# Low parts of split weights: a negated high part and an adding transfer in place of a subtraction

## The chip, the cores and the metric

The kernel runs on one core of a Trainium2 chip. The metric is device time in microseconds (us), the median of three runs. The core has five engines that work side by side, each through its own instructions in order: PE (TensorE, matmuls; PEld is its weight load), DVE (VectorE), ACT (ScalarE), POOL (GpSimd) and SP (SyncE, which here only issues transfers). Sixteen DMA engines move data between memory and the core's on-chip memory (SBUF); SP, ACT and POOL each have a queue that issues to them.

## The reference

One inference step of a hybrid diffusion backbone, two layers over 640 tokens (512 latent, 128 context) of 1024 features:

```
h  = RMSNorm(x) * (1 + scale1) + shift1
z  = h @ w_in                                # 6688 columns for all branches
x += gate1 * (sum_b sigmoid(G_b) * (branch_b @ w_b)) @ w_o   # linear attention, short convolution, Fourier mixing
h  = RMSNorm(x) * (1 + scale2) + shift2
gate, up = split(h @ w_up)
x += gate2 * (silu(gate) * up) @ w_down      # D_FF = 2816
```

The modulation vectors (shift, scale, gate) are `SiLU(cond) @ w_ada + b_ada`. All arrays are float32. The outputs are the normed tokens and the final attention states.

## The kernel before

**Products in three parts.** PE multiplies in a reduced format (fp32r). To keep float32 precision, each operand is split into a high part, the value cast to that format, and a low part, the value minus the high part. A product is then three matmuls of 128 x 128 weights by 320 tokens: high by high, high weight by low token, low weight by high token (`mm3`, lines 224 to 226, and `dense`, line 242). The third is the first that reads the low part of a weight.

**Weights.** `make_plan` lists all weights in the order of use. `_load` (line 132) brings them from memory through SP's queue into six buffers called raw, of 128 x 1024 values. `_split` (lines 136 to 142) makes a chunk's high part whi by a cast on ACT (line 140) and its low part wlo by a subtraction on DVE (line 141). There are three buffers each for whi and wlo, so chunk n can be split only when PE is done with chunk n - 3. `prefetch` splits up to two chunks ahead of the one in use.

**Kinds of chunk.** A "full" chunk is one block of output columns: `wb` (branch outputs, 512 columns wide here), `wo` (1024), `wd` (products down, 384 or, in the last group of a layer, 512), and a few of `w1` and `wu` (1024). A "pair" is two blocks that go through the seven products of Strassen and Winograd in place of eight; its two raw tiles give four chunks: *a* (line 156, the first raw tile as it is, 1024 columns), *b* and *c* (sums and differences of the quarters, made by DVE at lines 162 to 168 in tiles sb and sc), and *d* (line 171, one quarter, 512 columns, in one buffer of its own, whi2 and wlo2). There are 24 pairs a layer in the mixer (`w1p`) and 19 in the feed-forward phase (`wup`, blocks 3 to 21). "Raw" chunks (`w_ada`) are used as they are.

**Order.** The feed-forward phase goes by chunks of three blocks up (the last has four); the eight products down of one chunk stand between the next chunk's blocks up: three behind the first, three behind the second, two behind the third, or two behind each of four. The framework's scheduler sets the order of instructions on each engine, and each engine runs its list in order. Mixer and feed-forward phase are joined by `boundary`, where the last blocks and the next phase's first go by halves of the tokens, with two or three chunks held at once. The tile z gathers a pair's products on DVE (lines 269 to 279); ff and ffhi are the feed-forward activations and their high parts (ACT).

Of the kernel before, what the change touches and what calls it, by code (L numbers as in the profile page):

```python
# [11 lines left out]
F32 = mybir.dt.float32  # L12
F32R = mybir.dt.float32r
U8 = mybir.dt.uint8
AF = mybir.ActivationFunctionType
# [29 lines left out]
N_UNITS = 47  # L45
# [3 lines left out]
def ffn_order():  # L49
    """The blocks of the second residual branch: those of one chunk's products down stand between the next's up."""  # L50
# [9 lines left out]
def ada_after(l, phase, i):  # L60
    """The quarters of modulation vectors made after the i-th block of a phase."""
# [31 lines left out]
class Builder:  # L93
# [42 lines left out]
    def _split(self, src, n, small=False):  # L136
        c, sfx, b = (512, "2", 1) if small else (1024, "", 3)
# [3 lines left out]
        self.nc.vector.tensor_sub(lo[:, 0:n], src, hi[:, 0:n].bitcast(F32))  # L141
        return hi, lo

    def _prep(self, c):
# [4 lines left out]
        if stage == "f":  # L149
            n = self.plan[i][2][0].shape[1]  # L150
            self.hl[c] = self._split(self.raw.pop((i, 0))[:, 0:n], n)
            self.freed += 1
            return
        r1, r2 = self.raw[i, 0], self.raw[i, 1]
        a11, a12, a21, a22 = r1[:, 0:512], r1[:, 512:1024], r2[:, 0:512], r2[:, 512:1024]
        if stage == "a":
            self.hl[c] = self._split(r1, 1024)
# [12 lines left out]
        else:  # L170
            self.hl[c] = self._split(a22, 512, True)
# [14 lines left out]
    def prefetch(self, ahead):  # L186
        """Splits the weights that come next, up to some chunks ahead of the last taken."""
# [57 lines left out]
    def pair(self, key, h, T12, T34):  # L245
        """Two blocks of 128 columns over 8 blocks of the features and both halves of the tokens by the
        seven products of Strassen and Winograd; the two results, each [P, 2, TH]."""
# [112 lines left out]
    def ada(self, pieces):  # L360
        """Quarters of modulation vectors; what follows the products comes one piece later."""
# [13 lines left out]
    def table(self, name):  # L375
        """Loads a table set behind the functions of the one before."""
        self.in_order(lambda: self.tc.keep_in_program_order(self.nc.scalar.preload_act_table_set(name)))

    def act(self, *args, **kw):
        """A function that not all table sets have."""  # L380
# [45 lines left out]
    def modulate(self, half, r, xs, A, sh, out, hx):  # L426
        """Yields after each feature block's part of h."""
# [52 lines left out]
    def boundary(self, keys, rhs, xs, g, after_x, norm, head, gk=None, tail=3):  # L480
        """The blocks that end a residual branch, the norm, and the blocks that start the next phase.

        The last few of the former and all of the latter go by halves of the tokens, so that the norm of
# [675 lines left out]
```

## Time and profile before

| | |
|---|---|
| Time, median of 3 runs | 2075.63 us (2074.26 to 2076.05) |
| Profiled execution: span from first to last instruction | 2075.0 us |
| PE busy | 2012.5 us, 97% |
| DVE busy | 1570.5 us, 76% |
| ACT busy | 919.4 us, 44% |
| POOL busy | 18.2 us, 1% |
| Read from memory and written | 227.69 MB and 26.74 MB |

The profile is that of one execution; its span is 0.6 us below the median of the runs. Busy time is the time in which an engine had an instruction at work. PE is busy nearly throughout; an engine that is busy less than PE costs nothing unless PE waits for it.

### The profile page before, as it was taken

How to read it: one execution, taken by the hardware profiler on the slowest of the kernel's cores; microseconds unless marked ns; L12 is line 12 of the kernel's file. 1: busy time of each engine (PE TensorE's matmuls, PEld its weight loads, DVE VectorE, ACT ScalarE, POOL GpSimd, SP SyncE). 2: the span in 40 equal slices, each digit the busy share in tenths (PEclk: the TensorE clock that was granted, in tenths of full speed). 3: DMA queues.
4: the chain of work that ended last, by engine and by line, in shares of the span. 5: the costliest groups of instructions: out<-in, count | busy, mean ns of one | idle time of the engine just before them, and what ended most of it. 6: DMA issues, size and time to landing. Idle time of an engine off the chain costs nothing. (4 is left out here: it accounts for less than half of the span.)

```text
span 2075.0 us, 35216 instructions
## 1 busy us (share of the span) xinstructions
PE 2012.5 (97%) x14100; PEld 1936.3 (93%) x14100; DVE 1570.5 (76%) x2508; ACT 919.4 (44%) x1445; POOL 18.2 (1%) x52
## 2 busy tenths in 40 slices
PE   5999999999999999999999999999999999999997
PEld 2999998999999999999979999899999999999997
DVE  5778798877667777777677878898765787877876
ACT  5554435445445333333365454544543643333333
POOL 2000000000000000000000000000000000000000
PEclk9999999999999999999999999999999999999999
DMA  8254442554612333333232453335545222222222
GB/s 320 69 171 136 148 140 95 186 197 141 210 55 62 103 118 98 105 114 103 83 126 84 165 171 132 118 129 173 192 153 173 62 64 78 78 92 71 88 72 71
DMA packets 107139, 256.72 MB, mean 124 GB/s; under 512 B 13344, under 2 KB 46304, under 8 KB 106976
## 3 DMA queue, kind: packets, MB, share of 16 engines
q1 hardware_dynamic: 102528, 250.91, 36.8%
q8 instruction: 111, 1.82, 0.4%
q10 hardware_dynamic: 3728, 2.49, 0.4%
q0 software_dynamic: 720, 1.07, 0.1%
q14 instruction: 52, 0.43, 0.1%
HBM read 227.69 MB, written 26.74 MB: 123 GB/s over the span
## 5 line engine op out<-in xcount | busy, mean ns | idle before, releaser
L140 ACT CAST whi<-raw 128x1024 fp32r<-128x1024 f32 (+2 forms) x368 | 270.1, 734 | 529.5 <-PE wo L242 37.3
L141 DVE TENSOR_TENSOR wlo<-raw,whi 128x1024 fp32r<-128x1024 f32 (+2 forms) x368 | 304.4, 828 | 112.2 <-ACT whi L140 111.8
L242 PE MATMUL wd<-ffhi,whi 128*128 128x320 f32 x656 | 150.2, 310 | 0.0
L242 PE MATMUL wd<-fflo,whi 128*128 128x320 f32 x656 | 149.5, 309 | 0.0
L242 PE MATMUL wd<-ffhi,wlo 128*128 128x320 f32 x656 | 149.4, 309 | 0.0
L140 ACT CAST whi<-sb 128x1024 fp32r<-128x1024 f32 x86 | 90.3, 1050 | 125.7 <-PE wd L242 31.5
L140 ACT CAST whi<-sc 128x1024 fp32r<-128x1024 f32 x86 | 90.3, 1050 | 107.8 <-PE wd L242 48.0
L141 DVE TENSOR_TENSOR wlo<-sc,whi 128x1024 fp32r<-128x1024 f32 x86 | 104.9, 1220 | 30.2 <-ACT whi L140 29.6
L473 DVE SCALAR_TENSOR_TENSOR x<-wd,mod,x 128x512 f32<-128x512 f32 x212 | 106.7, 545 | 23.0 <-PE wd L242 23.0
L242 PEld LDWEIGHTS wd<-ffhi,whi 128*128 128x128 f32 x656 | 109.4, 188 | 3.3 <-ACT whi L140 3.3
L141 DVE TENSOR_TENSOR wlo<-sb,whi 128x1024 fp32r<-128x1024 f32 x86 | 104.8, 1219 | 6.8 <-ACT whi L140 6.7
L242 PEld LDWEIGHTS wd<-ffhi,wlo 128*128 128x128 f32 x656 | 109.7, 188 | 0.0
L242 PEld LDWEIGHTS wd<-fflo,whi 128*128 128x128 f32 x656 | 109.6, 188 | 0.0
L162 DVE TENSOR_TENSOR sc<-raw 128x512 f32<-128x512 f32 x86 | 59.3, 689 | 27.3 <-DMA raw<-in_w 26.0
L342 PE MATMUL ada<-raw,cond 128*32 128x256 f32 x768 | 56.5, 410 | 9.2 <-ACT cond L381 5.5
L163 DVE TENSOR_TENSOR sb<-sc,raw 128x512 f32<-128x512 f32 x86 | 59.1, 687 | 0.5
L168 DVE TENSOR_TENSOR sc<-raw,sb 128x512 f32<-128x512 f32 x86 | 59.1, 687 | 0.3
L242 PE MATMUL wb<-bhi,whi 128*128 128x320 f32 x256 | 59.2, 312 | 0.0
L164 DVE TENSOR_TENSOR sb<-raw,raw 128x512 f32<-128x512 f32 x86 | 59.0, 686 | 0.0
L242 PE MATMUL wb<-bhi,wlo 128*128 128x320 f32 x256 | 58.4, 309 | 0.0
L242 PE MATMUL wb<-blo,whi 128*128 128x320 f32 x256 | 58.3, 309 | 0.0
L342 PEld LDWEIGHTS ada<-raw,cond 128*32 128x32 f32 x768 | 20.8, 114 | 31.7 <-issue 7.2
(2254 smaller groups left out, 6417.0 us busy)
## 6 DMA issues: line engine op xcount, KB each, us to landing
raw<-in_w SPq DMA_DIRECT2D x104, 512.0 KB, 4.4
raw<-in_w_ada SPq DMA_DIRECT2D x96, 512.0 KB, 3.8
raw<-in_wu SPq DMA_DIRECT2D x88, 512.0 KB, 3.6
raw<-in_wd SPq DMA_DIRECT2D x96, 192.0 KB, 2.3
sgd<-z SPq DMA_DIRECT2D x48, 320.0 KB, 3.1
sgl<-sgd SPq DMA_DIRECT2D x48, 320.0 KB, 3.8
raw<-in_wb SPq DMA_DIRECT2D x48, 256.0 KB, 2.8
raw<-in_wo SPq DMA_DIRECT2D x16, 512.0 KB, 3.5
```

Source lines behind the costliest of these rows:

```text
L140: self.nc.scalar.copy(hi[:, 0:n], src)
L141: self.nc.vector.tensor_sub(lo[:, 0:n], src, hi[:, 0:n].bitcast(F32))
L162: nc.vector.tensor_add(sc[:, 0:512], a21, a22)
L163: nc.vector.tensor_sub(sb[:, 0:512], sc[:, 0:512], a11)
L164: nc.vector.tensor_sub(sb[:, 512:1024], a11, a21)
L168: nc.vector.tensor_sub(sc[:, 512:1024], a12, sb[:, 0:512])
L242: nc.tensor.matmul(o[h], w[:, sl], rhs[kb][h][part], start=(kb == 0 and first), stop=(kb == nk - 1 and last))
L342: self.nc.tensor.matmul(ps[32 * j:32 * j + 32, 0:256], self.cond[:, 4 * kp + j, :], r[:, j, :], start=(kp == 0), stop=(kp == 1))
L473: self.nc.vector.scalar_tensor_tensor(seg(xv), seg(v), g[:, j, i:i + 1], seg(xv), ALU.mult, ALU.add)
```

## The change

A low part of a weight that is used as it stands in memory (full chunks, and *a* and *d* of a pair) is no longer a subtraction on DVE. ACT writes the negated high part into wlo (a second pass behind the cast), and a transfer on POOL's queue adds the weights from memory to it in place. The *b* and *c* chunks, which are sums, keep the subtraction. The *d* chunk's buffers go from one to two each, and the pool of work tiles from 47 to 45. (Removed comments are left out here; line numbers of the changed kernel are 6 higher behind `_split`.)

```diff
-N_UNITS = 47
+N_UNITS = 45
...
-    def _split(self, src, n, small=False):
-        c, sfx, b = (512, "2", 1) if small else (1024, "", 3)
+    def _split(self, src, n, small=False, dram=None):
+        c, sfx, b = (512, "2", 2) if small else (1024, "", 3)
         hi = self.wp.tile([P, c], F32R, tag="whi" + sfx, name=self.name("whi"), bufs=b)
         lo = self.wp.tile([P, c], F32R, tag="wlo" + sfx, name=self.name("wlo"), bufs=b)
         self.nc.scalar.copy(hi[:, 0:n], src)
-        self.nc.vector.tensor_sub(lo[:, 0:n], src, hi[:, 0:n].bitcast(F32))
+        if dram is None:
+            self.nc.vector.tensor_sub(lo[:, 0:n], src, hi[:, 0:n].bitcast(F32))
+        else:
+            self.nc.scalar.activation(lo[:, 0:n], hi[:, 0:n].bitcast(F32), AF.Copy, scale=-1.0)
+            self.nc.gpsimd.dma_start(lo[:, 0:n], dram, accum_op=ALU.add)
         return hi, lo
...
-            self.hl[c] = self._split(self.raw.pop((i, 0))[:, 0:n], n)
+            self.hl[c] = self._split(self.raw.pop((i, 0))[:, 0:n], n, dram=self.plan[i][2][0])
...
-            self.hl[c] = self._split(r1, 1024)
+            self.hl[c] = self._split(r1, 1024, dram=self.plan[i][2][0])
...
-            self.hl[c] = self._split(a22, 512, True)
+            self.hl[c] = self._split(a22, 512, True, dram=self.plan[i][2][1][:, 512:1024])
```

The order of ACT before, in the second layer's feed-forward phase, from the last of three blocks down ahead of pair 7 (raw_317) to the casts of pair 7 itself (raw_318_0 is its *a*, raw_318_1 its *d*):

```order
L140 CAST whi_2574_18342<-raw_317_0_18082 128x384
L140 CAST whi_2588_18430<-raw_318_1_18225 128x512
L381 ACTIVATE ff_2557_18215<-z_2563_18230 128x640
L140 CAST whi_2577_18369<-raw_318_0_18114 128x1024
L301 CAST ffhi_2572_18338<-ff_2557_18215 128x640
L140 CAST whi_2582_18399<-sb_2580_18394 128x1024
L140 CAST whi_2586_18426<-sc_2581_18395 128x1024
```

The same place on ACT after, where raw_322_1 is the *d* chunk of pair 8:

```order
L142 CAST whi_2574_18634<-raw_317_0_18369 128x384
L146 ACTIVATE wlo_2575_18635<-whi_2574_18634 128x384
L387 ACTIVATE ff_2557_18504<-z_2563_18520 128x640
L142 CAST whi_2616_18938<-raw_322_1_18729 128x512
L142 CAST whi_2577_18662<-raw_318_0_18402 128x1024
L307 CAST ffhi_2572_18630<-ff_2557_18504 128x640
L146 ACTIVATE wlo_2578_18663<-whi_2577_18662 128x1024
L142 CAST whi_2582_18693<-sb_2580_18688 128x1024
L146 ACTIVATE wlo_2617_18939<-whi_2616_18938 128x512
L142 CAST whi_2586_18720<-sc_2581_18689 128x1024
```

The negation of pair 7's *a* (wlo_2578) stands behind its cast and one cast of ffhi, and the *d* chunk of a pair is now cast one pair earlier, ahead of the next *a*.

On PE before, the end of the block down ahead of pair 7 and the pair's first products (hhl are the tokens):

```order
L242 MATMUL wd_1_1_2_2584_18403<-ffhi_2547_18156,wlo_2575_18343 128x320 x2
L224 MATMUL wup_1_7a_2592_18440<-hhl_2397_17089,whi_2577_18369 128x320
L225 MATMUL wup_1_7a_2592_18440<-hhl_2397_17089,whi_2577_18369 128x320
L226 MATMUL wup_1_7a_2592_18440<-hhl_2397_17089,wlo_2578_18370 128x320
L224 MATMUL wup_1_7a_2592_18440<-hhl_2399_17096,whi_2577_18369 128x320
```

On PE after, the same place:

```order
L248 MATMUL wd_1_1_2_2584_18697<-ffhi_2547_18444,wlo_2575_18635 128x320 x2
L230 MATMUL wup_1_7a_2592_18735<-hhl_2397_17359,whi_2577_18662 128x320
L231 MATMUL wup_1_7a_2592_18735<-hhl_2397_17359,whi_2577_18662 128x320
L230 MATMUL wup_1_7b_2593_18736<-hhl_2418_17466,whi_2577_18662 128x320
L231 MATMUL wup_1_7b_2593_18736<-hhl_2418_17466,whi_2577_18662 128x320
L232 MATMUL wup_1_7a_2592_18735<-hhl_2397_17359,wlo_2578_18663 128x320
```

Two products with the high part of the pair's second block stand ahead of the first that reads the low part.

## Rows read from the trace of the kernel before

**Rows 1.** Page, busy time of the engines: us (share of the span), instructions.
```profile
PE 2012.5 (97%) x14100; PEld 1936.3 (93%) x14100; DVE 1570.5 (76%) x2508; ACT 919.4 (44%) x1445; POOL 18.2 (1%) x52
```

**Rows 2.** Stages: stretch and length, busy per engine (instructions), clock, DMA share, GB/s.
```profile
50.00:450.00 400.00, 392.09 (x2817) 370.40 (x2818) 325.68 (x507) 190.23 (x291) 3.66 (x13) 0.99 0.42 141
1100.00:1450.00 350.00, 340.27 (x2484) 321.83 (x2483) 290.92 (x451) 169.23 (x258) 3.67 (x13) 1.00 0.42 142
...
625.00:1050.00 425.00, 423.34 (x2955) 416.81 (x2954) 315.46 (x491) 158.91 (x228) 0.00 (x0) 1.00 0.33 103
1650.00:2050.00 400.00, 398.34 (x2717) 398.07 (x2716) 306.66 (x457) 149.97 (x210) 0.00 (x0) 1.00 0.25 76
```

**Rows 3.** Waits of PE: for whom, us in total, times, longest.
```profile
PE w1p_17a L224 <- DVE z L279: 4.1, 2, 2.3
...
PE w1p_36a L224 <- DVE z L279: 2.9, 2, 1.5
```

**Rows 4.** Groups of instructions: shapes, count, busy us, mean ns, idle before.
```profile
L140 ACT CAST whi<-raw 128x1024 fp32r<-128x1024 f32 x122 | 127.8, 1049 | 161.5 <-PE wo L242 37.3 <-PE wd L242 13.0 <-PE wu L225 6.5
L140 ACT CAST whi<-raw 128x512 fp32r<-128x512 f32 x150 | 92.9, 619 | 147.8 <-PE wb L242 35.0 <-PE wd L242 17.8 <-PE w1p_8d L225 7.1
...
L141 DVE TENSOR_TENSOR wlo<-raw,whi 128x1024 fp32r<-128x1024 f32 (+2 forms) x368 | 304.4, 828 | 112.2 <-ACT whi L140 111.8
```

**Rows 5.** Timeline of ACT, feed-forward phase: start, length, instruction, idle before.
```profile
1724.86 1.05 ACT L140 CAST whi<-raw 128x1024 fp32r<-128x1024 f32 x1 [3.00 <-PE wup_5d L225]
...
1742.46 0.51 ACT L140 CAST whi<-raw 128x384 fp32r<-128x384 f32 x1 [3.00 <-PE wup_6d L225]
...
1746.76 1.05 ACT L140 CAST whi<-raw 128x1024 fp32r<-128x1024 f32 x1 [0.79 <-PE wd L242]
1747.71 0.73 ACT L301 CAST ffhi<-ff 128x640 fp32r<-128x640 f32 x1
```

**Rows 6.** Chain that ended last, the blocks down there: start, length, matmuls.
```profile
1726.73 5.28 PE wd L242 x36
1744.33 7.92 PE wd L242 x54
```

**Rows 7.** Transfers: a queue's bytes and share; issues, KB each, us to landing.
```profile
q1 hardware_dynamic: 102528, 250.91, 36.8%
...
raw<-in_wu SPq DMA_DIRECT2D x88, 512.0 KB, 3.6
...
raw<-in_wb SPq DMA_DIRECT2D x48, 256.0 KB, 2.8
...
w_gk<-in_w_gk POOLq DMA_DIRECT2D x2, 256.0 KB, 6.4
```

**Rows 8.** Timeline of POOL: issue of a transfer, start and length.
```profile
5.00 0.54 POOL L331 DMA_DIRECT2D w_gk<-in_w_gk  x1
```

**Rows 9.** Two pauses of PE in the mixer, and PE's clock behind each.
```profile
296.51 0.63 PE L224 MATMUL w1p_17a<-hhl,whi 128*128 128x320 f32 x1 [2.27 <-DVE z L279]
...
296.00:298.00 2.00, 1.49 (x5) 0.59 0.97 391
298.00:300.00 2.00, 2.00 (x10) 0.56 0.01 2
...
1318.13 0.41 PE L224 MATMUL w1p_17a<-hhl,whi 128*128 128x320 f32 x1 [1.86 <-DVE z L279]
...
1318.00:1320.00 2.00, 1.86 (x13) 1.00 0.98 397
```

**Rows 10.** Timelines of ACT and DVE at the first layer's boundary into feed-forward.
```profile
604.75 1.04 ACT L140 CAST whi<-raw 128x1024 fp32r<-128x1024 f32 x1
...
605.83 1.23 DVE L141 TENSOR_TENSOR wlo<-raw,whi 128x1024 fp32r<-128x1024 f32 x1
```

**Rows 11.** Mixer: cast of a pair's chunk on ACT, and the pair's products.
```profile
1434.28 1.05 ACT L140 CAST whi<-raw 128x1024 fp32r<-128x1024 f32 x1 [1.23 <-PE w1p_12b L225]
...
L224 PE MATMUL w1p_14a<-hhl,whi x8: 309/309/309, 424.6 to 1444.5; 128*128 128x320 f32 x8
```

## Prediction

> **What bounds the kernel now.** I read the page's head first, then busy time by stage, then PE's waits. PE is busy for 2012.5 of the 2075.0 us [rows 1], so a change that takes no matrix work away can win at most the rest. By stage [rows 2] the two stretches of the mixer's projections have PE at 392.09 of 400 and 340.27 of 350 us: 17.6 us of idle time in 750. The feed-forward stretch (625 to 1050, and 1650 to 2050) has 1.66 us of idle time in each layer, nearly all of it at its start. DVE is busy for 74 to 83% of these stretches and ACT for 37 to 48%, but PE rarely waits for DVE: the waits of PE that end on DVE's last sum of a pair (line 279) are 4.1 and 2.9 us, the largest of their kind [rows 3]. The low parts that the change takes from DVE (368 instructions, 304.4 us, [rows 4]) end no wait of PE that the view lists. So there is little to win, and the question is whether the new way to a low part is late.
>
> **The change, part by part.** *Removed:* 304.4 us of DVE work. It lies beside the products. It is worth something only where DVE's lag holds PE, in the 17.6 us above. I take 6 us of gain, about the 7.0 us of [rows 3] less what other work would still hold; the bounds are 0 and 17.6.
>
> *Added on ACT:* 368 negations. They read SBUF and write SBUF in the shapes of the casts, so I price them as those: 1.05 us for 1024 columns, 0.62 for 512 [rows 4]. ACT has the room for it by [rows 2]; what matters is that a negation stands between a cast and the transfer.
>
> *Added on POOL:* 368 transfers. Issuing one takes POOL 0.54 us [rows 8], some 199 us in all on an engine that is idle, so no queue builds up there.
>
> *The new chain.* A low part was there one cast (1.05) and one subtraction (some 1.2) after its buffer came free. Now it takes a cast, a negation, and a transfer from issue to landing, L. No row shows an accumulating transfer. The nearest is the plain load of the same 512 KB from SP in this stretch, 3.6 us [rows 7]. The queue's rows give 250.91 MB in 36.8% of 2075 us, or 329 KB per us on all 16 engines, so 524,288 bytes take 1.6 us of moving. Adding in place reads the destination too, which I price at the same 1.6; POOL's 0.54 goes on top. That is L = 3.6 + 1.6 + 0.54 = 5.75 us. From below, L is that of the plain load, 3.6. From above I take POOL's slowest plain transfer, 6.4 us for 256 KB at the crowded start [rows 7], plus 0.8 for the missing half and 1.6 for the second read: 8.8. I stay at 5.75, since the feed-forward stretch (DMA share 0.25 to 0.33, [rows 2]) is nearer to the loads there than to the start. The Trainium skill (DMA: Bandwidth & Descriptors, section on the anatomy of a DMA on the SWDGE path) gives such a transfer 2.0 us plus its bytes over 436 KB per us, which would be 3.2 us for 512 KB and 4.4 if the second read counts as bytes; no row of before shows a quiet POOL transfer, and with 4.4 the sum below would end near 2109.
>
> *Where it is late.* A buffer of high and low parts comes free when the third chunk before it is done, so the chain must fit into two chunks of PE's work. In the feed-forward phase a chunk of the products down takes 2.64 us (54 matmuls in pairs, 7.92 us, are three of them, [rows 6]). Where three such blocks stand ahead of a pair, the pair's first chunk *a* (1024 columns) may be cast only when the first of the three is done. The trace has this: block group at 1744.33, cast of *a* at 1746.76, pair at 1744.33 + 7.92 = 1752.25 [rows 5, 6]. In the new order the cast of the *d* chunk of the pair after stands ahead of it, and needs a load whose buffer, as I read the order, the cast at 1742.46 sets free; with 3.6 us of load it ends some 0.45 us past 1746.76, so *a* starts at 1747.2. Cast 1.05, in about half of these places the cast of ffhi (0.73, which the row at 1747.71 shows right behind it), negation 1.05, L 5.75: the low part lands at 1755.05, or 1755.78 with ffhi. The first product that needs it is the pair's third, at 1752.54; where the order has pulled two high products of the next block forward, at 1752.83. The stall is 2.5 to 2.95 us, say 2.7. There are ten such pairs in a layer (blocks 4, 5, 7, 8, 10, 11, 13, 14, 16, 17): 20 x 2.7 = 54 us.
>
> Where two blocks stand ahead, *a* takes the buffer of the previous pair's *c*: cast at 1724.86, blocks from 1726.73 for 5.28, so the pair starts at 1732.01 [rows 5, 6]. 1724.86 + 1.05 + 1.05 + 5.75 = 1732.71 against 1732.30 for the third product: 0.4 us, eight pairs a layer, 6.5 us in all.
>
> *Phase boundaries.* At the start of a phase two or three chunks of 1024 columns are cast while the next blocks wait for all of them. The second of them is cast at 604.75 and its subtraction ends at 605.83 + 1.23 = 607.06 [rows 10]; now it lands at 604.75 + 1.05 + 1.05 + 5.75 = 612.6, or 5.5 us later. The order lets the products of the other blocks run first, so I take 4 us for each of three boundaries, 12 us (bounds 0 and 24).
>
> *The clock.* A pause of 2.27 us ahead of 296.51 was followed by a granted clock of 0.59 and 0.56 for four microseconds (the level of 1.2 GHz), a pause of 1.86 us ahead of 1318.13 by none [rows 9]. The drop costs 1.49 x 0.41 + 2.00 x 0.44 = 1.5 us. I give it to half of the 20 long stalls: 15 us (bounds 0 and 54).
>
> *Where it stays hidden.* In the mixer a pair's *a* is cast at 1434.28; the last of the four products that open its steps starts at 1444.5 [rows 11], three steps of three matmuls (3 x 0.44) behind the first, so the third product is due at 1443.5. 1434.28 + 7.85 = 1442.1: 1.4 us of cover, and some 1 us more where modulation products stand between two pairs. The branch products wb take 512 columns: 0.62 + 0.62 + (2.8 + 0.8 + 0.54 = 4.1) = 5.4 us [rows 4, 7] against two chunks of 24 matmuls, each 4/3 of 2.64 = 3.52, so 7.04. The *d* chunks have two buffers now and a whole pair of time. The pool of work tiles has 45 buffers instead of 47; the order of PE shows some regrouping around two pairs of the mixer in layer 0 and no new wait that I can price. I cost all of these at nothing. If L is 8.8 in the mixer, its cover is gone: 1.7 us late, or 0.7 with modulation products ahead, some 1 us for each of 46 pairs.
>
> *Sum.* 54 + 6.5 + 12 + 15 - 6 = 81.5 us on the execution of 2075.0; the median lies 0.6 above it. 2075.6 + 81.5 = **2157 us**.
>
> **Rivals.**
> *Cheap transfer, still late.* The two reads run side by side and half of the second is hidden, and POOL's issue is inside the landing: L = 3.6 + 0.8 = 4.4. Then the long stalls are 1.35 us each, 27; the short ones vanish; boundaries 8, clock 5, gain 6: 34 us, 2109. With L = 3.6 the stalls are 0.55 each, 11, boundaries 6, no clock, gain 6: 11 us, 2087. For it speaks that loads in this stretch land in 3.6; against it, that POOL's rows at the start are all above 5.
>
> *Faster.* If the transfer lands within 3.0 us, the chain at 1747.2 + 2.1 + 3.0 = 1752.3 meets the third product and nothing stalls. What is left is DVE's relief, at most 17.6 us: 2058, and with 6 to 10 us of it some 2068. It decides at L = 3.0, and the 3.6 of a plain load speaks against it.
>
> *Crowded transfers.* The change reads the weights a second time. In a cycle of a pair and three blocks (12.3 + 7.9 us) the new transfers move 2 x 1.34 MB, or 8.2 us of all 16 engines at the rate above, so the DMA share goes from about 0.3 to 0.7 there, and higher still in the mixer (0.42 before). If that makes L 8.8: long stalls 5.75 x 20 = 115, short ones 3.45 x 16 = 55, boundaries 21, clock after all 36, 54, mixer 46, branch products about 13, gain 6: 298 us, 2373.
>
> *It does not free anything.* DVE gets idle time, but PE's waits on line 279 stay, since they are set by PE's own products: the gain of 6 falls away, 2163. That is inside the forecast.
>
> **How the numbers follow.** Forecast (2110 to 2230): 0.44. Cheap transfer (2080 to 2110): 0.17. Crowded (2230 to 2375): 0.19, and beyond it 0.06. Faster by over 0.2% (under 2071.5): 0.08; within 0.2%, about what a measurement of this kernel can tell from no change (2071.5 to 2079.8): 0.06; slower: 0.86. The range from 2072 to 2340 leaves out the fast case (0.08), what lies beyond the crowded one (0.06) and its top quarter (0.05), together 0.19.
>
> **What would show it.** Right: PE's idle time in the feed-forward stretch rises from 1.7 us a layer to some 30 or more; PE's waits name wup blocks behind a DMA on wlo; the issue row of wlo shows some 5 to 6 us for 512 KB; the stalls stand at pairs behind three blocks, hardly at those behind two; DVE's busy time falls by 304 us, ACT's rises by some 290. Wrong: landings near 3 us, or no wait of PE on wlo in the feed-forward phase; stalls mainly in the mixer or in wb, which would mean crowding; or a clock that falls there (or never falls).

## The result and the profile after

| | before | after |
|---|---|---|
| Time, median of 4 runs each on one chip | 2075.84 us | 2292.7 us (2289.89 to 2297.36) |
| Ratio | | 1.105 (95% interval 1.103 to 1.107) |
| Span of the profiled execution | 2075.0 us | 2292.3 us |
| PE busy | 2012.5 us | 2081.4 us |
| PE idle (span less busy) | 62.5 us | 210.9 us |

The changed kernel takes 217 us longer. PE issues the same 14100 matmuls. Of the 217 us, 148 are new idle time of PE and 69 are matmuls that took longer.

The page after, busy time by engine (beside [rows 1]) and two of the DMA queues (packets, MB, share of 16 engines):

```profile
PE 2081.4 (91%) x14100; PEld 1983.1 (87%) x14100; DVE 1310.6 (57%) x2140; ACT 1171.8 (51%) x1813; POOL 340.1 (15%) x420
...
q1 hardware_dynamic: 102528, 250.91, 33.3%
q0 software_dynamic: 53712, 123.25, 33.2%
```

DVE lost 259.9 us and ACT gained 252.4. The prediction had 304 and some 290 here. The second read is in q0: half of the bytes and half of the packets of q1, but as much transfer time.

The stages after, as in [rows 2] (stretch and length, busy per engine with instructions, granted clock, DMA share, GB/s):

```profile
50.00:450.00 400.00, 375.23 (x2682) 351.42 (x2679) 274.17 (x445) 225.38 (x337) 46.37 (x62) 0.98 0.68 183
...
625.00:1050.00 425.00, 372.15 (x2424) 360.43 (x2424) 215.80 (x356) 188.89 (x296) 67.53 (x77) 0.94 0.60 135
1650.00:2050.00 400.00, 363.31 (x2325) 357.68 (x2324) 203.95 (x333) 196.64 (x306) 64.69 (x74) 0.94 0.65 145
```

In the first of the two feed-forward stretches PE was idle for 1.7 of 425 us; now it is for 53, and the clock of the stretch is 0.94 instead of 1.00.

Waits of PE after (for whom, us in total, times, longest):

```profile
...
PE wu L232 <- DMA wlo<-in_wu: 8.8, 2, 5.4
PE wup_5a L232 <- DMA wlo<-in_wu: 8.5, 2, 5.2
PE w L248 <- DMA wlo<-in_w: 8.4, 3, 6.3
PE wup_7a L232 <- DMA wlo<-in_wu: 8.1, 2, 4.2
PE wup_13a L232 <- DMA wlo<-in_wu: 7.4, 2, 4.0
...
PE wup_11a L232 <- DMA wlo<-in_wu: 7.0, 2, 4.8
PE wb L248 <- DMA wlo<-in_wb: 6.7, 7, 2.3
PE wd L232 <- DMA wlo<-in_wd: 6.6, 3, 3.8
PE wup_4a L232 <- DMA wlo<-in_wu: 6.6, 2, 3.7
PE wup_16a L232 <- DMA wlo<-in_wu: 6.4, 2, 4.0
PE wup_10a L232 <- DMA wlo<-in_wu: 6.0, 2, 3.8
PE wup_17a L232 <- DMA wlo<-in_wu: 6.0, 2, 3.6
PE wu L248 <- DMA wlo<-in_wu: 5.8, 2, 3.1
PE wup_14a L232 <- DMA wlo<-in_wu: 5.3, 2, 2.7
...
PE w L232 <- DMA wlo<-in_w: 5.0, 2, 2.5
PE w1p_36a L230 <- DVE z L285: 4.9, 2, 2.5
PE wup_8a L232 <- DMA wlo<-in_wu: 4.7, 2, 2.3
PE wo L248 <- DMA wlo<-in_wo: 4.1, 2, 2.8
...
PE w1p_16a L232 <- DMA wlo<-in_w: 3.5, 2, 1.9
...
PE wup_9a L232 <- DMA wlo<-in_wu: 2.6, 2, 1.7
...
PE w1p_17a L230 <- DVE z L285: 0.3, 2, 0.2
```

Most of the long waits are for a low part on its way from memory; the longest of all, 11.5 us at the start, was 10.7 before. The ten pairs of a layer behind three blocks down sum to 66.0 us, 3.3 each; the eight behind two to 13.4 us, 0.8 each. Of the waits on DVE's sums in [rows 3], that of w1p_17a fell from 4.1 to 0.3 us, while that of w1p_36a grew from 2.9 to 4.9 and that of w1p_44b from 2.0 to 3.1: with w1p_10a (0.5 and 0.3) 9.5 us in all before, 8.6 after.

One long stall, pair 7 of the second layer, in the chain that ended last (start, length, piece):

```profile
1912.58 4.77 DMA raw<-in_wu
1917.60 0.36 issue
1917.95 1.04 ACT whi L142
1919.00 0.63 ACT ffhi L307
1919.62 0.97 ACT wlo L146
1920.59 0.28 issue
1920.88 5.40 DMA wlo<-in_wu
...
1926.32 0.63 PE wup_7a L232
1926.95 0.27 PE wup_7a L230
...
1929.09 0.27 PE wup_7a L232
...
1929.58 0.15 PE wup_7b L230
```

This is the chain that the prediction described: a load for the d chunk ahead, the cast, ffhi, the negation, POOL's issue, the landing, then PE, which had been idle for 3.90 us. Behind the stall a matmul takes 0.27 us for some 3 us, then 0.15 again. The granted clock in the same place:

```profile
1926.00:1928.00 2.00, 1.68 (x6) 1.68 (x7) 1.50 (x3) 0.00 (x0) 0.00 (x0) 0.50 0.68 121
1928.00:1930.00 2.00, 2.00 (x11) 2.00 (x10) 0.00 (x0) 0.42 (x1) 0.00 (x0) 0.65 0.29 88
1930.00:1932.00 2.00, 2.00 (x16) 2.00 (x15) 0.00 (x0) 1.04 (x2) 0.00 (x0) 1.00 0.00 0
```

0.50 is the level of 1.2 GHz. The drop costs 1.68 x 0.50 + 2.00 x 0.35 = 1.5 us, as in [rows 9].

The same sum over all stretches of 2 us (PE's busy time, times what the clock lacks to 1.00) gives 62.4 us after and 6.5 before, so 56 of the 69 us of longer matmuls are the clock's. Behind the first 50 us, alike in both kernels, there are 29 places with a lowered clock after, worth 59.1 us, and 2 before. Sixteen stand behind the 20 long waits, one behind a pair with two blocks ahead of it (pair 15, 3.21 us), twelve elsewhere, most of them at phase boundaries. A place costs 1.4 to 3.4 us, 2.0 in the mean: behind some the clock stayed down for longer, and in some a second wait came close behind the first. Not every wait of this length is followed by a drop: 2.89 us ahead of pair 4 in layer 0 was not (first row), 2.19 ahead of pair 11 in layer 1 was (second row):

```profile
722.00:724.00 2.00, 1.89 (x13) 1.89 (x14) 0.00 (x0) 0.12 (x1) 0.00 (x0) 1.00 0.00 0
2022.00:2024.00 2.00, 2.00 (x9) 2.00 (x9) 0.00 (x0) 0.42 (x1) 0.00 (x0) 0.50 0.35 98
```

The other 13 us aren't in the granted clock. A matmul that starts behind a pause takes 0.31 us or more in the trace where one in a chain adds 0.15, and PE has 103 pauses over 0.2 us instead of 38, so some 10 us of it may be that (an estimate from these rows).

Issues after (KB each, median us to landing), beside [rows 7]:

```profile
wlo<-in_w POOLq DMA_DIRECT2D x56, 512.0 KB, 7.3
wlo<-in_wu POOLq DMA_DIRECT2D x50, 512.0 KB, 5.7
...
wlo<-in_wd POOLq DMA_DIRECT2D x96, 192.0 KB, 4.4
```

In what follows one more measure is used. The first matmul that reads a low part of pair 4, and the one of pair 21, bound the same work in every kernel. Rows of before and of after (the two times are the first start, in layer 0, and the last, in layer 1; first is taken from first and last from last):

```profile
L226 PE MATMUL wup_4a<-hhl,wlo x8: 309/309/309, 675.7 to 1695.6; 128*128 128x320 f32 x8
L226 PE MATMUL wup_21a<-hhl,wlo x8: 309/309/309, 1009.9 to 2018.6; 128*128 128x320 f32 x8
```

```profile
L232 PE MATMUL wup_4a<-hhl,wlo x8: 309/441/636, 722.1 to 1858.5; 128*128 128x320 f32 x8
L232 PE MATMUL wup_21a<-hhl,wlo x8: 309/309/417, 1116.0 to 2233.3; 128*128 128x320 f32 x8
```

Pairs 4 to 21 took 334.2 and 323.0 us, now 393.9 and 374.8: 111.5 us of the 217. The other half lies elsewhere, at the phase boundaries and in the mixer.

### The profile page after: what moved, and what is told of

The parts are those of the page before. It is cut to its first block, busy times and chain, and to the rows that moved or that the text cites. A ratio compares the mean times of both kernels' runs of the same rounds, so it can differ in the third digit from the quotient of the medians.

```text
span 2292.3 us, 36236 instructions
## 1 busy us (share of the span) xinstructions
PE 2081.4 (91%) x14100; PEld 1983.1 (87%) x14100; DVE 1310.6 (57%) x2140; ACT 1171.8 (51%) x1813; POOL 340.1 (15%) x420
## 3 DMA queue, kind: packets, MB, share of 16 engines
q1 hardware_dynamic: 102528, 250.91, 33.3%
q0 software_dynamic: 53712, 123.25, 33.2%
## 4 chain that ended last, share of the span: by engine, by line
PE 44%; issue 22%; DMA 19%; ACT 6%; POOL 3%; DVE 3%; POOLq 0%; ACTq 0%; SPq 0%; DVEq 0%
DMA wlo<-in_wu 10%; DMA wlo<-in_w 4%; PE wb L248 3%; POOL wlo L147 3%; PE wu L248 2%; ACT whi L142 2%; PE wd L248 2%; ACT wlo L146 2%; DMA raw<-in_wu 2%; DMA wlo<-in_wd 1%; DVE S L673 1%; DMA sgd<-z 1%; PE o L694 1%; PE ada L348 1%; ACT dup L929 1%
## 5 line engine op out<-in xcount | busy, mean ns | idle before, releaser
L142 ACT CAST whi<-raw 128x512 fp32r<-128x512 f32 (+2 forms) x368 | 268.9, 733 | 484.3 <-DMA raw<-in_wu 44.6
L146 ACT ACTIVATE wlo<-whi 128x512 fp32r<-128x512 f32 (+2 forms) x368 | 272.7, 744 | 9.0
L147 POOL DMA_DIRECT2D wlo<-in_w x104 | 91.0, 878 | 727.0 <-ACT wlo L146 660.5
L147 POOL DMA_DIRECT2D wlo<-in_wd x112 | 98.0, 875 | 545.0 <-ACT wlo L146 490.9
L147 POOL DMA_DIRECT2D wlo<-in_wu x88 | 78.8, 907 | 337.4 <-ACT wlo L146 333.1
L147 POOL DMA_DIRECT2D wlo<-in_wb x48 | 41.9, 874 | 188.8 <-ACT wlo L146 166.1
```

The lines of the kernel that those rows point to most:

```text
L142: self.nc.scalar.copy(hi[:, 0:n], src)
L146: self.nc.scalar.activation(lo[:, 0:n], hi[:, 0:n].bitcast(F32), AF.Copy, scale=-1.0)
L147: self.nc.gpsimd.dma_start(lo[:, 0:n], dram, accum_op=ALU.add)
```

## The experiments

All edits are made to the changed kernel unless said otherwise; "4 to 21" is the measure above, for both layers.

### Undoing one part

**No transfer.** The negation stays and the transfer goes.

```diff
-            self.nc.gpsimd.dma_start(lo[:, 0:n], dram, accum_op=ALU.add)
```

> The changed kernel without the adding transfers: the low part stays the negated high part, so the low parts are left out of the computation; casts, negations and their order rules stay. Theory 1 (the chain cast, negation, transfer is too long for two chunks of PE's work): without the transfer the chain is 2.1 us, shorter than before, so no wait of PE on wlo and 2065 to 2085 us. Rival 'ACT' (273 us of extra passes, and casts of d chunks put ahead of casts of a chunks, are what delays): the time stays above 2150. Rival 'traffic' (second read of the weights crowds the DMA engines): also 2065 to 2085.

Measured: 2081.97 us, 1.004 (1.003 to 1.006) of before; 4 to 21: 334.5 and 323.0. That is what the theory and the rival 'traffic' had; the rival 'ACT' falls. The negations, the new order and the smaller pools cost 9 us; all else, some 210 us, comes with the transfers. DVE has 1310.0 us of work instead of 1570.5, and nothing is gained by it. (The low parts are left out of this kernel's result.)

**The a chunks by subtraction.**

```diff
-            self.hl[c] = self._split(r1, 1024, dram=self.plan[i][2][0])
+            self.hl[c] = self._split(r1, 1024)
```

> Only the a chunks of the 86 pairs go back to the subtraction; full chunks and d chunks keep negation and transfer. Theory 1: the waits of PE on wup a chunks (93 us in the profile after) and on w1p a chunks (13 us) go, with the clock loss behind them; the boundaries (some 40 us of waits) stay: 2120 to 2150. Rival 'traffic': a chunks are 45 of 123 MB of the new transfers, so some 0.37 of the 217 us goes: 2200 to 2220.

Measured: 2162.29 us, 1.042 (1.040 to 1.044); 4 to 21: 337.8 and 323.0. The a chunks carry 130 us. What is left, some 90 us against before on the same chip (2072.74), is more than the theory allowed and less than the rival did. The waits stand on the wide full chunks (wu 11.0 + 8.6, w 8.0 + 5.0), on wd (6.3 + 4.0) and on wb (9.6). The expectation read the waits on the a chunks of wup as 93 us; the rows after sum to 79.4 (66.0 + 13.4).

**All chunks of 1024 columns by subtraction.**

```diff
-        if dram is None:
+        if dram is None or n > 512:
```

> Edit: chunks of 1024 columns (a, and the wide full chunks of w, wu and wo) get their low parts by subtraction again; negation and transfer stay for chunks of 512 columns or less (wd, wb, d). Beside the run that gave subtraction back to a alone (2162 us), this tells what the wide full chunks at the phase boundaries cost. Theory: some 40 us of waits there and 10 to 15 of clock, so 2098 to 2118, with waits left on wd and wb of some 10 us each. Rival (boundaries are late for another reason, such as ACT's order or the loads): 2145 or more.

Measured: 2105.29 us, 1.015 (1.014 to 1.017), clock 0.990. That is inside the theory's range. So the wide full chunks at the phase boundaries cost 2162.3 - 2105.3 = 57 us, their clock included. Left are wb with 10.5 us of waits and wd with some 6.

**The d chunks alone by transfer.** Full chunks and a by subtraction.

```diff
-            self.hl[c] = self._split(self.raw.pop((i, 0))[:, 0:n], n, dram=self.plan[i][2][0])
+            self.hl[c] = self._split(self.raw.pop((i, 0))[:, 0:n], n)
...
-            self.hl[c] = self._split(r1, 1024, dram=self.plan[i][2][0])
+            self.hl[c] = self._split(r1, 1024)
```

> Edit: negation and transfer for the d chunks alone (two buffers, 45 work tiles); all other low parts by subtraction as before. A d chunk has a whole pair of PE's time for its chain. Theory (only the chain's length against its cover counts): hidden, no wait on these low parts, 2070 to 2084, the upper part if the cast ahead of a and the 45 work tiles cost what they did without any transfer. Rival (an adding transfer costs PE something wherever it runs, by its traffic): above 2095.

Measured: 2078.94 us, 1.003 (1.002 to 1.004), and no wait of PE on a low part, as the theory had it. 86 adding transfers of 256 KB that land in 4.0 to 4.7 us are hidden, since a whole pair covers them. It is still 0.3% slower than before; nothing here beats the subtraction.

### Lateness or traffic

**Traffic without lateness.** Subtraction as before, without the negation and with one d buffer, and each adding transfer goes into a tile that nobody reads.

```diff
-            self.nc.scalar.activation(lo[:, 0:n], hi[:, 0:n].bitcast(F32), AF.Copy, scale=-1.0)
-            self.nc.gpsimd.dma_start(lo[:, 0:n], dram, accum_op=ALU.add)
+            self.nc.vector.tensor_sub(lo[:, 0:n], src, hi[:, 0:n].bitcast(F32))
...
+            self.nc.gpsimd.dma_start(self.dummy[:, o:o + n], dram, accum_op=ALU.add)
```

> The subtraction on DVE is back (buffers of d: one, work tiles: 45), but the same 368 adding transfers of the same bytes still run on POOL's queue, into a tile that nothing reads. Theory 1: PE waits for no transfer, 2075 to 2095. Rival 'traffic': loads and stores get as late as in the changed kernel, 2150 or more. Rival 'ACT': 2075 to 2095, since the negations are gone.

Measured: 2571.28 us. By the total that is the rival's side (2150 or more), but for another reason, and the total can't be used: the transfers waited for each other's half of the one tile on POOL, and short writes of the attention state queued behind them, so that PE's two largest waits name DVE (278.5 us) and POOL (148.8), neither a weight. But pairs 4 to 21 of the first layer are clean:

```profile
922.00:1256.00 334.00, 334.00 (x2347) 327.74 (x2346) 248.69 (x384) 116.70 (x168) 59.47 (x68) 1.00 0.76 176
```

These pairs run from 922.1 to 1256.3 us, 334.2 us as before. In that time 68 adding transfers (of earlier weights, since POOL's queue is behind) move 23.9 MB, where the changed kernel moves 21.8 MB by adding in the same pairs; the DMA share is 0.76 instead of 0.60 to 0.65, plain loads of wu land in 5.6 us instead of 3.8, and PE is busy all the time at a clock of 1.00. So the second read's traffic, without lateness, costs these pairs nothing. (In the second layer, 323.0 us, the transfers had run out.)

**Transfers for wide chunks alone, then lateness without traffic.** First the other half of the narrow run; then the same with each transfer replaced by five, six or seven writes on GpSimd, about 1 us each.

```diff
-        if dram is None:
+        if dram is None or n < 1024:
...
-            self.nc.gpsimd.dma_start(lo[:, 0:n], dram, accum_op=ALU.add)
+            for k in range(5):
+                self.nc.gpsimd.memset(lo[:, 0:n].bitcast(F32), 0.001)
```

> Edit: the other half of the narrow run: negation and transfer for the chunks of 1024 columns alone (a and the wide full chunks), subtraction for wd, wb and d. In its order no d cast stands ahead of the next a. Expected from the runs so far (2292 less some 30 for wd and wb, less some 15 for d): 2235 to 2270, the feed-forward stretches of both layers nearly as long as in the changed kernel, clock there 0.93 to 0.96.

> Edit: as the run before it, with each adding transfer replaced by five writes of a constant over the low part on GpSimd, about 1.0 us each (a 640-column write takes 0.64), some 5.3 us with the hand-over: the low part is as late as by a transfer of the feed-forward phase, and nothing is read from memory. The weights' low parts are left out of the result. Theory (lateness alone makes the loss, and the clock's loss follows PE's idle time): the stretch 625 to 1050 has as much work done as in the run with transfers, within 6 us of PE's busy time at full speed, with a clock of 0.93 to 0.96 there; total 2190 to 2260 (the mixer's and boundaries' transfers take longer than 5.3, so somewhat less is lost there). Rival (the second read's traffic slows PE, its loads or the clock): clock 0.98 or more, less than half of the loss in that stretch, total below 2160.

> Edit: as the run with five writes on GpSimd, with six. One write took 0.95 us and five of them 5.10 us from the end of the negation to PE's start, where the transfers of the run wide took 5.92 for the same pair; six give 6.1. The weights' low parts are left out of the result. Theory (lateness alone): behind three blocks down PE waits 1.3 to 2.3 us on the low part as it did for the transfers, clock 0.95 to 0.97 in the stretch 625 to 1050, total 2155 to 2200. Rival (traffic): the clock stays at 0.98 or more though the waits are there, and the total is below 2150.

> Edit: the same with seven writes, 7.1 us from the negation to PE: a little later than the feed-forward phase's transfers and nearly as late as the mixer's. The weights' low parts are left out of the result. Theory: waits behind three blocks down of 2.3 to 3.3 us, clock 0.94 to 0.96 there, total 2200 to 2270, on both sides of the 2232 of the run with transfers. Rival (traffic): clock 0.97 or more there and below 2190.

| run | from negation to PE, pair 7 | time, us | PE busy | clock of the run | 4 to 21, us |
|---|---|---|---|---|---|
| wide (transfers) | 5.92 us | 2231.71 | 2064.4 | 0.970 | 382.2, 362.7 |
| five writes | 5.10 us | 2128.65 | 2036.4 | 0.987 | 345.1, 334.2 |
| six writes | 6.12 us | 2173.77 | 2050.4 | 0.981 | 358.1, 345.6 |
| seven writes | 7.13 us | 2218.3 | 2072.7 | 0.974 | 366.7, 350.8 |

The first column is read from the chains: in wide the negation ends at 1873.62 and PE starts at 1879.54, with five writes at 1790.13 and 1795.23; each further write adds 1.0 us. Each write on the 122 wide chunks adds 45 us of time and lowers the clock, with not one byte more from memory: lateness alone costs 54 us with five writes and 144 with seven, and the clock falls with it.

The expectations came out unevenly. Wide is 3 us below its range. Five writes came out as their rival had it (below 2160, clock 0.99 in the stretch from 625 to 1050), six inside the theory's total but with a clock of 0.98 there, seven as the theory had it (2218, clock 0.96). So lateness costs, but less than the transfers do: six writes are as late as a transfer in the feed-forward phase and cost 47 us in pairs 4 to 21 (24 + 23) where the transfers cost 88. Traffic isn't the difference, by the run above. The waits of the run with seven writes and of wide on the same pair show what is (start, length, instruction, idle before it; the first two rows are of seven writes):

```profile
1875.74 0.41 PE L233 MATMUL wup_7c<-thi,wlo 128*128 128x320 f32 x1 [0.51 <-DVE wlo L144]
1877.78 0.41 PE L233 MATMUL wup_7a<-hhl,wlo 128*128 128x320 f32 x1 [0.31 <-POOL wlo L148]
```

```profile
1879.54 0.41 PE L232 MATMUL wup_7a<-hhl,wlo 128*128 128x320 f32 x1 [2.49 <-DMA wlo<-in_wu]
```

With the writes in the program, the scheduler put products with the pair's c chunk ahead of the low part on PE, in this pair four with five writes, seven with six and fourteen with seven; with a transfer it put none there, as if the transfer were short (how it reckons a transfer's length isn't on record). So PE's fixed order looks like a second cause, and it gets its own run at the end (the last of the next part).

### The chain against its cover

**One d buffer.** The next pair's d cast can then not stand ahead of a.

```diff
-        c, sfx, b = (512, "2", 2) if small else (1024, "", 3)
+        c, sfx, b = (512, "2", 1) if small else (1024, "", 3)
```

> Edit: the d chunk's buffers go back from two to one each; all else as in the changed kernel. The cast of the next pair's d can then no longer stand ahead of the next a on ACT. Theory (chain length): in the changed kernel that cast waits for its load behind three blocks down, some 1.7 us of the long stalls; without it the ten pairs a layer behind three blocks wait about 1.5 us each instead of 3.3, with less clock loss: 2240 to 2270, sum of the waits on their low parts 25 to 45 us instead of 66. Rival (the transfer alone makes the stall, or traffic does): within 8 us of 2292, waits of 60 us or more.

Measured: 2313.26 us, 1.114 (1.111 to 1.117): slower by 21 us than with two, against the theory and its rival. The pair's own d chunk is now split right ahead of a, its transfer runs beside a's, and the landing of a went from 5.7 to 7.3 us:

```profile
wlo<-in_wu POOLq DMA_DIRECT2D x50, 512.0 KB, 7.3
```

So the edit changed two things at once; the next two runs part them.

**d by subtraction, with two buffers and with one.**

```diff
-            self.hl[c] = self._split(a22, 512, True, dram=self.plan[i][2][1][:, 512:1024])
+            self.hl[c] = self._split(a22, 512, True)
```

> Edit: the d chunks alone get their low part by subtraction again (two buffers kept, so the next pair's d is still cast ahead of the next a); a and full chunks keep negation and transfer. Takes 86 transfers of 256 KB and their negations out. Theory (company): a transfer of 512 KB lands later when a d transfer is under way beside it, 5.7 us to landing falls by 0.5 us or more, 2255 to 2278. Rival (the load that the d cast waits for is what makes the long stalls late, the transfers hardly matter): 2280 to 2292, with the waits behind three blocks down still 3 us or more each.

> Edit: as the run before it, with one buffer for d instead of two, so that the d cast of a later pair cannot stand ahead of the next a on ACT and no d transfer is in the way either. Theory (the cast in front, waiting for its load, costs some 1.6 us of each long stall): the waits behind three blocks down fall by 1.2 us or more each against the two-buffer run, and the time by 25 to 45 us. Rival (it costs nothing, since the transfer's own landing decides): within 8 us of the two-buffer run.

Measured: 2280.38 us with two buffers (1.100, 1.098 to 1.101) and 2272.76 with one (1.096, 1.095 to 1.098). The d transfers cost 12 us. Both times the rival's numbers came out, barely: 2280.38 where the first had 2280 to 2292, and 7.6 us apart where the second had 8. The reason that the first rival gave, the cast's load, doesn't stand beside the second. The d cast in front costs next to nothing: without it the long stalls sum to 52.9 instead of 60.4 us, but the pairs behind two blocks to 23.2 instead of 15.1. In pair 7 the cast that waited for its load is gone, and the stall fell only from 3.64 to 2.72 us, with 5.87 us of landing instead of 5.21. The theory that this cast makes the long stalls is dropped; what is left of the chain is the landing. With one buffer, where d's transfer goes out right ahead of a's, the median landing for wu is 5.9 us without d transfers and 7.3 with them; with two it is 5.5 and 5.7.

**Two transfers of 512 columns** for a low part of 1024.

```diff
-            self.nc.gpsimd.dma_start(lo[:, 0:n], dram, accum_op=ALU.add)
+            for c0 in range(0, n, 512):
+                cs = slice(c0, min(c0 + 512, n))
+                self.nc.gpsimd.dma_start(lo[:, cs], dram[:, cs], accum_op=ALU.add)
```

> Edit: a low part of 1024 columns is added by two transfers of 512 columns, one behind the other, so a pair's first product (columns 0 to 511) waits for 256 KB only. Theory (the landing of 512 KB is the price, and part of it grows with the bytes): the first half lands in some 4.9 us, as the d chunks do, 0.8 us sooner; 20 long stalls, the boundaries and the mixer's a chunks get shorter by about that much: 2250 to 2280. Rival (a fixed price of an adding transfer, or POOL's issue, which doubles): no gain, 2285 to 2330.

Measured: 2222.47 us, 1.071 (1.068 to 1.073), a gain of 70 us, more than expected. In the chain of pair 7 the first half lands in 3.88 us, against 5.40 for the whole:

```profile
1869.76 3.88 DMA wlo<-in_wu
```

The long stalls fall from 66 to 41 us, 4 to 21 to 374.1 and 350.7.

**Four buffers**, three chunks ahead, five raw buffers for the room, one d buffer; and its control, the same with every low part by subtraction.

```diff
-        while self.loaded < min(len(self.loads), self.freed + 6):
+        while self.loaded < min(len(self.loads), self.freed + 5):
...
-        c, sfx, b = (512, "2", 2) if small else (1024, "", 3)
+        c, sfx, b = (512, "2", 1) if small else (1024, "", 4)
...
-        self.prefetch(2)
+        self.prefetch(3)
```

> Edit: four buffers instead of three for high and low parts, split up to three chunks ahead instead of two, one buffer again for d, five raw buffers instead of six (for the room). Same transfers, same bytes. Theory (chain length against two chunks of cover): one more chunk of cover, 2.6 us in the feed-forward phase behind blocks down and more elsewhere, so the long stalls of 3.3 us fall below 1, the short ones go, boundaries halve, and the clock there comes back to 0.97 or more: 2110 to 2160. Rival (traffic of the second read, contention): waits stay as they are, above 2240. Five raw buffers may add waits for loads of 0 to 30 us to either.

> Edit: the control for the run with four buffers: the same four buffers, five raw buffers, one d buffer and three chunks ahead, with every low part by subtraction and no transfer. If the 80 to 90 us that the four-buffer run still loses come from the transfers (mixer and boundaries): 2070 to 2090. If they come from the fifth raw buffer less and the order that follows: 2120 or more.

Measured: 2163.42 us (1.044, 1.040 to 1.048), 3 us above the theory's range, and 2077.76 for the control (1.003, 1.002 to 1.004). The feed-forward phase is almost cured, though the landing of wu got longer (6.5 us) and the DMA share is 0.69; the stretch from 625 to 1050:

```profile
625.00:1050.00 425.00, 416.32 (x2865) 407.30 (x2864) 254.02 (x416) 224.87 (x346) 79.57 (x91) 0.99 0.69 156
```

4 to 21 takes 338.4 and 328.1 us, 9 us more than before instead of 111.5. This is the plainest answer: the same transfers, the same bytes, one more chunk of cover. The control shows that the 86 us that this run still loses come with negations and transfers and not with the buffers; all but 9 of them lie outside these pairs.

**Four buffers and two halves.**

> Edit: four buffers, three chunks ahead, five raw buffers, one d buffer, and 1024 columns in two transfers of 512: both edits that shortened the loss. Theory (lateness against cover): the rest of 2163 lies in the mixer and at its start, where transfers of 512 KB land in 7 us and more; a first half that lands 1.5 us sooner gives 2110 to 2150. Rival (what is left there is not the landing but the added work on ACT and the traffic): 2155 to 2175.

Measured: 2161.34 us (2153.51 to 2184.4), 1.043 (1.037 to 1.050): no better than four buffers alone, and in the rival's range (added work on ACT, and traffic). So what is left there isn't the landing of 512 KB. PE is busy for 374 of 400 us in the mixer in both runs, and its waits spread over many lines (the start, w 5.3 us; d chunks of single pairs 2.5 to 3.7; ACT's copies of s 4 to 5). ACT's work alone can hardly be it, since the run without transfers kept that and lost 9 us, but neither part of the rival was tested here: the cause was not found.

**High products first.** Of an a chunk, the 16 products with the high part, then the eight with the low part.

```diff
-        prod(pa[:, 0:TH], w, 0, B11)
-        nc.scalar.copy(s1, pa[:, 0:TH])
-        prod(pb[:, 0:TH], w, 512, B21)
+        ab = [(o, c0 + kb * P, *ops[kb], kb) for o, c0, ops in ((pa[:, 0:TH], 0, B11), (pb[:, 0:TH], 512, B21)) for kb in range(4)]
+        for o, c, rh, rl, kb in ab:
+            nc.tensor.matmul(o, w[0][:, c:c + P], rh, start=kb == 0, stop=False)
+            nc.tensor.matmul(o, w[0][:, c:c + P], rl, start=False, stop=False)
+        for o, c, rh, rl, kb in ab:
+            nc.tensor.matmul(o, w[1][:, c:c + P], rh, start=False, stop=kb == 3)
+        nc.scalar.copy(s1, pa[:, 0:TH])
```

> Edit: the changed kernel with PE's order alone changed: of a pair's a chunk, all 16 products with the high part come first, then the eight with the low part, so 16 matmuls instead of 4 stand ahead of the first that reads the low part: 12 x 0.147 = 1.76 us more cover, with every transfer, wait and pass on ACT as it was. Theory (lateness against the cover that PE's order gives): the 20 long stalls fall from 3.3 to about 1.5 us, the 16 short ones and the mixer's go, some 58 us of waits, and with the clock's share of 0.46 per us of idle time 85 us: 2195 to 2225, and pairs 4 to 21 of a layer shorter by 30 us or more. Rival (PE's order doesn't matter, the transfers' traffic does): above 2270.

Measured: 2225.08 us, 1.071 (1.069 to 1.073): 68 us less than the changed kernel, at the upper edge of the expected range. 4 to 21 takes 364.5 and 339.7 us, 29 and 35 less. The long stalls sum to 28 us, 1.4 each, where 1.5 was expected. Twelve matmuls more ahead of the first low product take away what twelve matmuls last. PE's busy time fell only from 2081.4 to 2070.9 us, so less of the clock came back than the share of 0.46 promised. With the same transfers and the same landing (5.7 us for wu), PE's order is thereby shown to be a cause of its own.

### The clock

**Fill.** Ahead of the pairs behind three blocks down, 20 matmuls of no use, so that PE works where it would wait.

```diff
+        if key[0] == "wup" and key[2] % 3 and 3 < key[2] < 18:
+            for k in range(N_FILL):
+                nc.tensor.matmul(pc[:, 512:512 + TH], B22[k % 4][0][:, 0:P], B22[k % 4][0], start=True, stop=True)
```

> The changed kernel with 20 more matmuls (2.9 us at full clock, their result not used) on PE ahead of each feed-forward pair behind three blocks down, where PE waits some 3.3 us for the a chunk. Theory 'clock' (the pauses lower the granted clock, and that costs the 69 us that PE's busy time grew by): the pauses are shorter, the clock stays up in the feed-forward stretch (0.99 or more instead of 0.95), and 35 to 55 us go: 2235 to 2260. Rival (matmuls are slower for another cause, such as transfers into the same memory): the clock stays at 0.95 there and the time at 2285 to 2300.

Measured: 2272.17 us, 1.096 (1.094 to 1.098). 400 matmuls more, and 20 us less time: between the theory's range and the rival's, but the sign is that of the clock. Row of the second layer's feed-forward phase:

```profile
1650.00:2050.00 400.00, 375.88 (x2501) 370.08 (x2500) 206.96 (x334) 198.50 (x304) 65.94 (x76) 0.98 0.65 147
```

The clock is 0.98 there instead of 0.94. The profile gives the fill 6.2 us for 40 matmuls, 62 us in all, so PE's own work took 2111.7 - 62 = 2050 us instead of 2081: 31 of the 69 us came back. That PE's pauses bring the lower clock, and with it a good part of the slower matmuls, is shown by this.

## Why the forecast went as it did

Slower was right, by the mechanism given, and the largest group of new waits stands where the prediction put it. The size was off: 81.5 us forecast, 217 measured, though inside the range. Term by term, from the profile after:

| term | forecast, us | measured, us |
|---|---|---|
| long stalls, 20 | 54 (2.7 each) | 66.0 (3.3 each) |
| short stalls, 16 | 6.5 (0.4 each) | 13.4 (0.8 each) |
| phase boundaries | 12 (3 places of 4 us) | 43.8, and 3.8 more on ff |
| mixer, a chunks | 0 | 12.5 |
| branch products wb | 0 | 6.7 |
| DVE's relief | -6 | 0 |
| clock | 15 (10 drops) | 56 (29 places with a lowered clock, 2 before) |
| slower matmuls beside the clock | none | 13 |
| sum | 81.5 | 215 of 217 |

- **L.** 5.75 us forecast, 5.7 measured in the feed-forward phase. The sum is right, and in part by luck: a plain load took 3.9 us there and not 3.6, POOL's issue 0.87 and not 0.54, which leaves 0.9 for the second read where 1.6 stood. No run measures the parts alone.
- **Long stalls.** Right place and nearly the size. The missing 0.6 us: the hand-over from ACT to POOL (0.28 in the chain) had no price, and the landing varies, 5.4 to 7.5 us ahead of these pairs. (Of the short stalls' 13.4 us, 4.9 stand at pairs 9 and 15 of the first layer, with landings of 7.8 and 9.4 us.) The d cast in front, 0.45 in the forecast, looked like 1.7 in one chain; the two runs with d by subtraction showed it worth 8 us in all.
- **The clock** is the step that failed most. The prediction gave a drop of 1.5 us to half of the 20 long stalls and to no other pause: 10 drops. The trace has 16 behind the long stalls and 13 elsewhere, the boundaries above all, and a place costs 2.0 us in the mean, not 1.5. The prediction priced waits of 4 us at the boundaries and gave them no drop, though in [rows 9] a pause of 2.27 us already had one.
- **Boundaries** failed next, by their number: not three places but eight, namely the first blocks of w and of wu, the wo blocks and the last blocks of wd in each layer, 43.8 / 8 = 5.5 us each. Full chunks, all but wd of them wide, stand there one behind another, and I priced only the one transition whose rows I had looked up. Removing the transfers of the wide ones gave 57 us, clock included. The 3.8 us on ff aren't the transfers': the run without them has that wait at 7.1 us too.
- **The mixer and wb**, taken as hidden by 1.4 us and 1.6 us, were not: a transfer of w lands in 7.3 us there, not 5.75, toward the 8.8 of the crowded rival, and one of wb in 5.8, not 4.1.
- **DVE's relief.** The rival that nothing is freed held in the sum: one wait on a pair's sum went, two others grew (9.5 us before, 8.6 after), and without transfers the kernel is 9 us slower than before.
- **The crowded rival** fell as a theory of the whole: L stayed at 5.7 in the feed-forward phase, where half of the loss and more is, a DMA share of 0.69 with one buffer more hardly cost anything there, and one of 0.76 without lateness cost nothing. In the mixer, where L was 7.3, it was half right. **The cheap transfer and the faster case** fell by L.
- **PE's order** was in view and undervalued: I counted two high products ahead of the first low one as given, though that order is itself part of the cost, 68 us of it.

## What to carry to other kernels

Moving work off an engine that nobody waits for gains nothing, and a longer chain in its place costs as soon as it is longer than its cover: count the buffers and the work between "buffer free" and "first read", at every phase boundary too. Price a stall of an otherwise busy PE with its clock: here each us of new idle time came with 0.3 to 0.9 us of slower matmuls (6.2 for 22.3 us in the run narrow, 24.8 for 65.5 with a by subtraction, 53.0 for 93.6 with halves, 69 for 148 in the changed kernel, 23.9 for 27.7 with five writes). If a late operand can't be made earlier, first put the products that don't need it ahead; here the scheduler did so by itself with the writes, but not with the transfers.

## What the runs showed of the hardware

- An adding transfer of 512 KB takes 5.7 us from POOL's issue to landing in the feed-forward phase and 7.3 in the mixer, where a plain load of 512 KB takes 3.9 and 5.0; POOL's own part of the issue is 0.87 us, against 0.54 for a plain one in [rows 8].
- The Trainium skill (DMA: Bandwidth & Descriptors, section on the anatomy of a DMA on the SWDGE path) fits 2.0 us plus the bytes over 436 KB per us, by which 512 KB would take an estimated 3.2 us. The trace has 5.7 to 7.3 for transfers that add, so here the measurement decides.
- A transfer for d right ahead lengthens the landing of a: with one d buffer, 512 KB of wu landed in 5.9 us (median) without transfers for d and in 7.3 with them; why isn't shown. The first of two halves of 256 KB landed in 3.88 us in one chain.
- Behind 16 of the 20 long waits of PE (2.2 to 5.2 us) the granted clock fell to 0.50 to 0.55 in some stretch of 2 us, behind the other four (2.3 to 2.9 us) it stayed at 1.00; a place with a lowered clock cost 2.0 us in the mean.
- The queue with the second read moved 123 MB and the one with the plain loads 251, in the same share of the DMA engines' time (33.2 and 33.3%): per byte an adding transfer occupied them twice as long.
